# Chaining four of a pair's seven products in one PSUM bank, spilling intermediates unsplit, and putting TensorE's pages at one offset

## The chip, the cores and the metric

The kernel runs on one core of one Trainium2 chip. The metric is the device time of one execution in microseconds (us). The kernel before takes 2529.87 us, the median of three runs (2528.91 to 2531.84).

## The reference

A decoder block over 2048 positions of 1024 channels in float32: an RG-LRU group and a gated short convolution side by side, then a gated feed-forward part with a convolution, and a last norm.

```python
h = rms_norm(x, norm1_g);  z = h @ w_in            # 1024 -> 3584
y_lru = rg_lru(causal_dwconv(lru_x, 4 taps) + b, two gates of 64x64 blocks per head) * gelu(lru_gate)
y_sc  = sc_b * causal_dwconv(sc_c * sc_x, 3 taps)
x = x + concat(y_lru, y_sc) @ w_out                # 1536 -> 1024
h = rms_norm(x, norm2_g)
u = causal_dwconv(h @ w_up, 3 taps)                # 1024 -> 6144, halves gate and up
x = x + (gelu(gate) * up) @ w_down                 # 3072 -> 1024
out = rms_norm(x, final_g)
```

## The kernel before, in words

Channels lie on the 128 partitions and positions along the free axis. The 2048 positions are worked in two halves of T = 1024, since the scan and the convolutions run forward in time; a PSUM bank holds 512 positions (NB). Every product is made of three matmuls of 128x128 by 128x512 in the fp32r type: each operand is split into a high part, copied by ScalarE (ACT, line 147), and a remainder, subtracted by VectorE (DVE, line 148), and TensorE (PE) adds high by high, high by low and low by high (lines 152 and 176).

The phases follow one another on PE: input products of half 0 (tiles zin) with the gates (zr, zi) between them, output projection of half 0 (o), the same two of half 1, then for each half the up products (za to zd) and the down projection (d). A projection runs over two blocks of 512 positions; in a block all eight banks collect 1024 output channels over 12 steps (o) or 24 steps (d) of 24 matmuls. An up phase takes 24 pairs of a gate and an up channel block; a pair's 2x2 block product is done with seven products of 12 matmuls in a Winograd form (lines 526 to 572): sums of weights S1 to S4 are made on DVE from each pair's raw weights (line 513), sums of activations T1 to T4 once in h_prep. Before, three of the seven products have banks of their own or share one, and the partial results are put together by ACT copies (line 554) and DVE additions (line 550).

The order of PE's and SyncE's (SP) instructions is the order in which the program writes them; ACT, DVE and GpSimd (POOL) are put in order by a scheduler, in which high_priority moves work ahead by 120 (HP) or 90 (HW) places. SP starts the loads in that order, and an instruction that waits there holds all behind it. Stores of intermediates go through POOL's queue: y (12 tiles a half) and f (24 tiles a half) are split first, and both parts are written to DRAM (spill, line 234) and read back per block as yb; x2, x3 and half 0 of the output also leave by POOL.

Memory of PE's operands is in pages of 4 KB per partition: 28 act pages, 9 w pages (split weights, and the residuals xr, x2r of a projection), 5 tmp pages, 4 buffers tagged u of 4108 bytes (convolution inputs, loads of x and x2, and yb), 2 raw buffers of 5x512. In the built program the w pages lie at byte 2912 modulo 4096, the act pages at 3040, and the four u buffers at 2912, 2944, 2976 and 3008. So the address of the weights less that of the moving operand, modulo 512, is 384 for zin and for the up products, 0 for the gates (both in act pages), and 0, 480, 448 or 416 in turn for o and d, whose moving operand yb goes round the u buffers.

The mean of squares (inv_rms, line 195) of a norm is split on ACT and DVE and summed over partitions by four matmuls with a constant matrix (tiles ms). For the norms b and c this is written after the second unit or pair of the following phase (lines 628, 646 and 662), in one piece.

## Time and profile before

| what | value |
|---|---|
| median of three runs | 2529.87 us (2528.91 to 2531.84) |
| profiled execution, its own time | 2526.32 us |
| its span in the trace | 2524.6 us |
| PE busy | 2448.6 us (97%), 10,414 matmul rows |
| DVE busy | 1635.4 us (65%) |
| ACT busy | 1041.4 us (41%) |
| POOL busy | 250.6 us (10%) |
| mean granted TensorE clock | 0.984 |
| bytes moved by DMA | 368.89 MB, 274.88 on q1 (SP's) and 92.29 on q0 (POOL's) |

Where the phases lie, from the trace (us from the start of the span): input half 0 to 363, output 0 to 498, input half 1 to 844, output 1 to 986.6, up 0 to 1475, down 0 to 1742.6, up 1 to 2229.9, down 1 to 2524.6. A matmul's row lasts about 395 ns while the next starts some 232 ns after it, so the start-to-start distance and not the row's length is what a matmul costs in a stream. A granted clock below 1 in a stretch says that some of its matmuls ran at a lower clock.

### The profile page before, as it was taken

To read this page: it belongs to the slowest core of one execution; us is meant where nothing else is said; L and a number is where in the kernel's file an instruction comes from. 1 tells how busy PE (TensorE), PEld (TensorE's weight loads), DVE (VectorE), ACT (ScalarE), POOL (GpSimd) and SP (SyncE) were. 2 spreads that over 40 slices of the span, in tenths; PEclk is the share of its full clock that TensorE was granted. 3 is DMA by queue.
4 is the path that set the end of the run, shared out by engine and by line. 5 is a ranking of instruction groups with operands and counts; after the bars stand their busy time and mean duration, and the time that the engine had idled before them with its cause. 6 is when DMAs were issued, how large, how long until landed. Compare 5 with 4: busy or idle time off the path is not lost.

```text
span 2524.6 us, 26774 instructions
## 1 busy us (share of the span) xinstructions
PE 2448.6 (97%) x10414; PEld 1974.2 (78%) x10414; DVE 1635.4 (65%) x1753; ACT 1041.4 (41%) x1108; POOL 250.6 (10%) x379
## 2 busy tenths in 40 slices
PE   7999999999999998899999999999899999999996
PEld 5888887877888877688888888787688888888785
DVE  8555664556655666788888863534788888853423
ACT  5554453354554333444444432222444444431211
POOL 3100110000000000122211200000110011100000
PEclk9999999999999999999999999999999999999998
DMA  4222337713213475223332356754223322368554
GB/s 148 91 68 78 120 111 279 250 63 104 96 63 109 175 274 192 84 100 117 108 109 100 112 191 227 277 209 168 84 110 108 117 100 104 113 257 295 184 184 163
DMA packets 120064, 368.89 MB, mean 146 GB/s; under 512 B 10368, under 2 KB 13568, under 8 KB 119936
## 3 DMA queue, kind: packets, MB, share of 16 engines
q1 hardware_dynamic: 94592, 274.88, 31.8%
q0 software_dynamic: 25344, 92.29, 9.6%
q8 instruction: 82, 1.34, 0.2%
q14 instruction: 46, 0.38, 0.0%
HBM read 270.66 MB, written 96.47 MB: 145 GB/s over the span
## 4 chain that ended last, share of the span: by engine, by line
PE 93%; DVE 3%; DMA 2%; issue 1%; ACT 1%; SPq 0%; DVEq 0%; ACTq 0%
PE zin_b L178 24%; PE d L153 20%; PE za L539 11%; PE zd L539 11%; PE zc L539 11%; PE o L153 10%; PE zb L539 5%; PE zi_b L178 1%; PE zr_b L178 1%; DMA ybo<-y_d 1%; DMA ybd<-f_d 0%; DVE cv L232 0%; DMA wr_d<-in_w_down 0%; DMA ha<-x_d 0%; DMA x<-in_xT 0%
## 5 line engine op out<-in xcount | busy, mean ns | idle before, releaser
L153 PE MATMUL d<-ybd,wh_d 128*128 128x512 f32 x1536 | 482.3, 395 | 6.0 <-DMA ybd<-f_d 3.7
L153 PEld LDWEIGHTS d<-ybd,wh_d 128*128 128x128 f32 x1536 | 289.4, 189 | 75.0 <-issue 5.2
L153 PE MATMUL d<-ybd,wl_d 128*128 128x512 f32 x768 | 303.2, 395 | 0.0
L148 DVE TENSOR_TENSOR wl_d<-wr_d,wh_d 128x1024 fp32r<-128x1024 f32 x96 | 115.8, 1223 | 280.4 <-ACT wh_d L147 252.9
L178 PE MATMUL zin_b<-xl,wh_in 128*128 128x512 f32 x896 | 282.8, 397 | 6.5 <-DVE xl L334 6.5
L178 PE MATMUL zin_b<-xh,wh_in 128*128 128x512 f32 x896 | 283.5, 397 | 1.3 <-ACT xh L333 0.9
L178 PE MATMUL zin_b<-xh,wl_in 128*128 128x512 f32 x896 | 282.2, 396 | 0.0
L153 PE MATMUL o<-ybo,wh_o 128*128 128x512 f32 x768 | 242.5, 397 | 6.5 <-DMA ybo<-y_d 4.2
L147 ACT ACTIVATE wh_d<-wr_d 128x1024 fp32r<-128x1024 f32 x96 | 97.1, 1053 | 332.1 <-DMA wr_d<-in_w_down 318.7
L178 PEld LDWEIGHTS zin_b<-xl,wh_in 128*128 128x128 f32 x896 | 169.7, 190 | 47.5 <-DVE xl L334 7.8
L178 PEld LDWEIGHTS zin_b<-xh,wh_in 128*128 128x128 f32 x896 | 170.1, 190 | 42.3 <-ACT xh L333 1.5
L178 PEld LDWEIGHTS zin_b<-xh,wl_in 128*128 128x128 f32 x896 | 169.6, 189 | 39.9
L153 PEld LDWEIGHTS o<-ybo,wh_o 128*128 128x128 f32 x768 | 145.1, 190 | 41.8 <-issue 3.9
L153 PEld LDWEIGHTS d<-ybd,wl_d 128*128 128x128 f32 x768 | 145.0, 189 | 33.3
L153 PE MATMUL o<-ybo,wl_o 128*128 128x512 f32 x384 | 152.2, 396 | 0.7 <-DVE wl_o L148 0.7
L513 DVE TENSOR_TENSOR wr_up<-wr_up 128x512 f32<-128x512 f32 x192 | 132.2, 689 | 3.2
L148 DVE TENSOR_TENSOR wl_in<-wr_in,wh_in 128x1024 fp32r<-128x1024 f32 (+1 forms) x62 | 72.7, 1177 | 91.2 <-PE zin_b L178 85.6
L539 PE MATMUL zc<-hhB,whd_up 128*128 128x512 f32 x384 | 128.0, 394 | 0.0
L232 DVE SCALAR_TENSOR_TENSOR cg<-ug,prm,cg 128x1024 f32<-128x1024 f32 x96 | 122.7, 1279 | 3.0 <-issue 2.8
L232 DVE SCALAR_TENSOR_TENSOR cu<-un,prm,cu 128x1024 f32<-128x1024 f32 x96 | 122.6, 1277 | 0.0
L539 PE MATMUL zd<-ht,wha_up 128*128 128x512 f32 x384 | 120.5, 395 | 0.0
L554 ACT ACTIVATE ug<-za 128x512 f32<-128x512 f32 x96 | 56.7, 591 | 126.3 <-PE za L539 126.3
(236 smaller groups left out, 4587.7 us busy)
## 6 DMA issues: line engine op xcount, KB each, us to landing
wr_up<-in_w_up SPq DMA_DIRECT2D x96, 512.0 KB, 4.6
wr_d<-in_w_down SPq DMA_DIRECT2D x48, 1024.0 KB, 7.6
ybd<-f_d SPq DMA_DIRECT2D x96, 512.0 KB, 4.9
wr_in<-in_w_in SPq DMA_DIRECT2D x54, 512.0 KB, 3.6
wr_o<-in_w_out SPq DMA_DIRECT2D x24, 1024.0 KB, 6.9
ybo<-y_d SPq DMA_DIRECT2D x48, 512.0 KB, 5.6
f_d<-cg POOLq DMA_DIRECT2D x48, 512.0 KB, 3.1
f_d<-cu POOLq DMA_DIRECT2D x48, 512.0 KB, 3.1
```

Of the source, the lines that this page charges most:

```text
L147: nc.scalar.activation(r32(hi), src, AF.Copy)
L148: nc.vector.tensor_tensor(r32(lo), src, hi, ALU.subtract)
L153: nc.tensor.matmul(ps, r32(a), r32(b), start=(first and i == 0), stop=(last and i == 2))
L178: nc.tensor.matmul(ps[t], r32(a), r32(b[:, blk(t)]), start=(first and i == 0), stop=(last and i == 2))
L232: nc.vector.scalar_tensor_tensor(dst, src[:, k : k + T], col(o_w + k), dst, ALU.mult, ALU.add)
L513: nc.vector.tensor_tensor(raw[:, o, :], raw[:, a, :], raw[:, b, :], ALU.add)
L539: nc.tensor.matmul(ps, r32(p[:, s]), r32(hs[k][x][o]), start=f and i == 0, stop=l and i == 2, skip_group_check=True,)
L554: nc.scalar.activation(dst, ps, AF.Copy)
```

## The change

Several things change together.

**Up products.** A class, Pair, takes the place of up_products. Bank x collects W11, then S2, S3 and W22 on top of one another; ACT copies it out after each of the four, so that the partial sums serve as the common parts of the results. W12 has bank a, S1 and S4 share bank c. DVE makes three additions a pair where it made five, ACT four copies where it made two. A copy of bank x must be done before the next product writes into x.

On PE the order of the products changes. In the rows below, which are the first matmul of each product in the middle of the first up phase, the tile ahead of the arrow is the bank, the first name behind it the moving operand, the last the weights (wha holds W22 and W12, whb W11 and S2, whc S3 and S1, whd S4). The kernel before, pair 11 and the start of pair 12:

```order
L539 MATMUL za0_11_8015<-hhB110_0_5689,whb_up0_11_7865 128x512
...
L539 MATMUL zb0_11_8016<-hhT10_0_5697,whb_up0_11_7865 128x512
...
L539 MATMUL zd0_11_8017<-hhB110_0_5689,whc_up0_11_7871 128x512
...
L539 MATMUL zc0_11_8018<-hhT10_0_5697,whc_up0_11_7871 128x512
...
L539 MATMUL za0_11_8015<-hhB210_0_5693,wha_up0_11_7859 128x512
...
L539 MATMUL zd0_11_8017<-ht0_0_5701,wha_up0_11_7859 128x512 x2
...
L539 MATMUL zc0_11_8018<-hhB210_0_5693,whd_up0_11_7875 128x512
...
L539 MATMUL za0_12_8152<-hhB110_0_5689,whb_up0_12_8002 128x512
```

The changed kernel at the same place, from W11 of pair 11 on (S4 of pair 11, in zc, follows the last row):

```order
L567 MATMUL zx0_11_7933<-hhB110_0_5631,whb_up0_11_7875 128x512
...
L567 MATMUL zc0_11_7961<-hhT10_0_5639,whc_up0_11_7881 128x512
...
L567 MATMUL zx0_11_7933<-hhT10_0_5639,whb_up0_11_7875 128x512
...
L567 MATMUL za0_11_8034<-hhB210_0_5635,wha_up0_11_7869 128x512
...
L567 MATMUL zx0_11_7933<-hhB110_0_5631,whc_up0_11_7881 128x512
...
L567 MATMUL zx0_12_8066<-hhB110_0_5631,whb_up0_12_8008 128x512
...
L567 MATMUL zx0_11_7933<-ht0_0_5643,wha_up0_11_7869 128x512 x2
...
L567 MATMUL zc0_12_8094<-hhT10_0_5639,whc_up0_12_8014 128x512
```

Between S2 and S3 in bank x stands one product (W12), between S3 and W22 one (W11 of the next pair); between W11 and S2 stand three.

**Intermediates.** Y and f cross DRAM as they are, once. A projection reads the 512 positions that it needs (256 KB a step) into the raw tile of the weights, which grows from 5 to 6 half pages, and splits them there on ACT and DVE; the split yb lies in w pages (act pages in down 1).

**Stores.** All of POOL's stores move to SP's queue. defer(n, ...) puts one in a list, and tick, which runs after each load of weights, starts it n loads later (4 for y, 1 for f, x2, x3 and the output).

**Pages.** The u buffers get a pool of their own, w has 10 pages, tmp 6, and the scratch space of the software DMA queue shrinks from 16384 to 1024 bytes. In the built program all act and w pages then lie at byte 3936 modulo 4096, so that the weights' address less the moving operand's is 0 modulo 512 in every product; the u buffers lie at 3936 to 4032 and TensorE reads none of them.

**Smaller ones.** For the norms b and c the split of the sums (mean_split) is written one unit or pair ahead of the ms matmuls, at priority HP. A gate's weights are loaded and split a unit ahead. The residuals xr and x2r lie in u buffers instead of w pages. Half 1's x_prep and both halves' h_prep run at other steps of the projections. In up_rest the up channel's convolution comes first.

SP's rows at the end of up 0 and the start of down 0 (wr is a raw tile, in_w_down the weights, f_d the spilled f, cu its source) read before:

```order
L504 DMA wr_up0_23_9500<-in_w_up 128x2x512 x2
L387 DMA wr_d0_0_0_9761<-in_w_down 128x2x1024
L414 DMA ybd0_0_0_9771<-f_d0_0_106 128x1024
L414 DMA ybd0_0_1_9797<-f_d0_1_107 128x1024
L387 DMA wr_d0_0_2_9823<-in_w_down 128x2x1024
```

and now:

```order
L532 DMA wr_up0_23_9461<-in_w_up 128x2x512 x2
L157 DMA f_d0_21_130<-cu0_21_9452 128x1024
L408 DMA wr_d0_0_0_9682<-in_w_down 128x2x1024
L410 DMA wr_d0_0_0_9682<-f_d0_0_109 128x512
L410 DMA wr_d0_0_0_9682<-f_d0_1_110 128x512
L157 DMA f_d0_22_131<-cu0_22_9585 128x1024
L157 DMA f_d0_23_132<-cu0_23_9664 128x1024
L408 DMA wr_d0_0_2_9750<-in_w_down 128x2x1024
```

The stores of the last two pairs' f now stand ahead of the load for steps 2 and 3. Down 1 has the same order. At the border between the two blocks of a projection (here output 0) the four x2 stores stand ahead of the second load of the new block:

```order
L408 DMA wr_o0_1_0_2898<-in_w_out 128x2x1024
L410 DMA wr_o0_1_0_2898<-y_d0_0_85 128x512
L410 DMA wr_o0_1_0_2898<-y_d0_1_86 128x512
L157 DMA x2_d0_0_157<-xr0_0_0_2745 128x2x512
L157 DMA x2_d0_1_158<-xr0_0_1_2747 128x2x512
L157 DMA x2_d0_2_159<-xr0_0_2_2749 128x2x512
L157 DMA x2_d0_3_160<-xr0_0_3_2751 128x2x512
L408 DMA wr_o0_1_2_2968<-in_w_out 128x2x1024
```

Before, these stores were POOL's, and SP went from the loads of steps 0 and 1 to the next ones. The diff, cut to its core:

```diff
+    ub = ctx.enter_context(tc.tile_pool(name="ub", bufs=1))
...
-    y_d = [[dr.tile([P, 2, 2, NB], F32, name=f"y_d{h}_{k}") for k in range(NOUT)] for h in range(NH)]
-    f_d = [[dr.tile([P, 2, 2, NB], F32, name=f"f_d{h}_{k}") for k in range(NFF)] for h in range(NH)]
+    y_d = [[dr.tile([P, T], F32, name=f"y_d{h}_{k}") for k in range(NOUT)] for h in range(NH)]
+    f_d = [[dr.tile([P, T], F32, name=f"f_d{h}_{k}") for k in range(NFF)] for h in range(NH)]
...
-        return page(name, "w", 9)
+        return page(name, "w", 10)
...
-        return page(name, "tmp", 5)
+        return page(name, "tmp", 6)
...
-        return sb.tile([P, T + 3], F32, name=name, tag="u", bufs=4)
+        return ub.tile([P, T + 3], F32, name=name, tag="u", bufs=4)
...
-        return sb.tile([P, 5, NB], F32, name=name, tag="wr", bufs=2)
+        return sb.tile([P, 6, NB], F32, name=name, tag="wr", bufs=2)
...
+    waiting = []
+
+    def defer(n, dst, src):
+        waiting.append([n, dst, src])
+
+    def tick():
+        for w in waiting:
+            w[0] -= 1
+        while waiting and waiting[0][0] <= 0:
+            _, dst, src = waiting.pop(0)
+            nc.sync.dma_start(dst, src)
+
...
-        return next(load_parts(src, name, 1))
+        out = next(load_parts(src, name, 1))
+        tick()
+        return out
...
-    def inv_rms(acc, name):
+    def mean_split(acc, name):
...
-        pss = [pst(f"ms_{name}_{t}") for t in range(0, n, NB)]
...
-        split(hi, lo, acc)
+        with tc.high_priority(offset=HP):
+            split(hi, lo, acc)
+        return hi, lo
+
+    def inv_rms(acc, name, parts=None):
+        n = acc.shape[-1]
+        hi, lo = parts or mean_split(acc, name)
+        pss = [pst(f"ms_{name}_{t}") for t in range(0, n, NB)]
...
-    def lru_gates(c, half, xc):
+    def gate_weights(c, half):
...
-        split(hi, lo, raw)
+        with tc.high_priority(offset=HW):
+            split(hi, lo, raw)
+        return hi, lo
+
+    def lru_gates(c, half, xc, gw):
...
-            product_step(ps, wcol((hi, lo), g), xc, True, True)
+            product_step(ps, wcol(gw, g), xc, True, True)
...
+        gw = gate_weights(0, half)
...
-                gates = lru_gates(c, half, xc)
+                gates = lru_gates(c, half, xc, gw)
+                if c + 1 < NLRU:
+                    gw = gate_weights(c + 1, half)
...
-            spill(y_d[half][n], *(v.rearrange("p (t c) -> p t c", t=2) for v in y))
+            defer(4, y_d[half][n], y)
...
-    def load_k2(src, k, name):
+    def load_k2(src, spilled, t, k, name, ypage):
...
-        flat_raw = flat(raw)
-        nc.sync.dma_start(flat_raw[:, : 2 * T].rearrange("p (k m) -> p k m", k=2), src[k : k + 2].rearrange("k p m -> p k m"))
+        w = raw[:, 0:4, :].rearrange("p (k a) c -> p k (a c)", k=2)
+        nc.sync.dma_start(w, src[k : k + 2].rearrange("k p m -> p k m"))
+        for i in range(2):
+            nc.sync.dma_start(raw[:, 4 + i, :], spilled[k + i][:, blk(t)])
+        tick()
...
+            yb = ypage(f"yb_{name}_{k + i}")
...
-                split(hi, lo, flat_raw[:, i * T : (i + 1) * T])
-            out.append((hi, lo))
+                split(yb[:, 0, :], yb[:, 1, :], raw[:, 4 + i, :])
+                split(hi, lo, w[:, i, :])
+            out.append(((hi, lo), yb))
...
-                    wts = load_k2(src, k, f"{name}{half}_{t}")
-                yb = sb.tile([P, 2, NB], F32, name=f"yb{name}{half}_{t}_{k}", tag="u", bufs=4)
-                nc.sync.dma_start(yb, spilled[k][:, t, :, :])
+                    wts = load_k2(src, spilled, t, k, f"{name}{half}_{t}", act if last_k else wpage)
+                wt, yb = wts[k % 2]
...
+    def res_page(name):
+        return ub.tile([P, 2, NB], F32, name=name, tag="u", bufs=4)
+
...
-            r = wpage(f"xr{half}_{t}_{i}")
+            r = res_page(f"xr{half}_{t}_{i}")
...
-        nc.gpsimd.dma_start(dst[:, :, blk(t)].rearrange("m p c -> p m c"), r)
+        defer(1, dst[:, :, blk(t)].rearrange("m p c -> p m c"), r)
...
+        tick()
...
-    def up_products(half, j, wt, hs):
...
+    class Pair:
+        def __init__(self, half, j, hs):
+            self.half, self.j, self.hs = half, j, hs
+            self.wt = up_weights(half, j)
+            self.x, self.a, self.c = None, None, None
...
+        def copy(self, dst):
+            with tc.high_priority(offset=HP):
+                nc.scalar.activation(dst, self.x, AF.Copy)
+
+        def add(self, dst, ps):
+            with tc.high_priority(offset=HP):
+                nc.vector.tensor_tensor(dst, ps, dst, ALU.add)
...
+        def begin(self):
+            n = f"{self.half}_{self.j}"
+            self.ug = with_halo(f"ug{n}", 2, self.half, u_halo[:, self.j, :])
+            self.un = with_halo(f"un{n}", 2, self.half, u_halo[:, NFF + self.j, :])
+            self.g = [self.ug[:, 2 + b * NB : 2 + (b + 1) * NB] for b in range(2)]
+            self.n = [self.un[:, 2 + b * NB : 2 + (b + 1) * NB] for b in range(2)]
+            self.x = pst(f"zx{n}")
+            self.run(self.x, "W11", "B11", True, False)
+            self.copy(self.g[0])
+
+        def sum1(self):
+            self.c = pst(f"zc{self.half}_{self.j}")
+            self.run(self.c, "S1", "T1", True, False)
+
+        def middle(self):
+            self.run(self.x, "S2", "T2", False, False)
+            self.copy(self.g[1])
+            a = pst(f"za{self.half}_{self.j}")
+            self.run(a, "W12", "B21", True, True)
+            self.add(self.g[0], a)
+            self.run(self.x, "S3", "T3", False, False)
+            self.copy(self.n[1])
+            self.add(self.n[1], self.c)
+
+        def fourth(self):
+            self.run(self.x, "W22", "T4", False, True)
+            self.copy(self.n[0])
+            keep_halo(self.un, 2, self.half, u_halo[:, NFF + self.j, :])
+
+        def end(self):
+            self.run(self.c, "S4", "B22", False, True)
+            self.add(self.g[1], self.c)
+            keep_halo(self.ug, 2, self.half, u_halo[:, self.j, :])
...
+        conv(cu, un, 3, O_FCW + 3 * (NFF + j))
...
-        conv(cu, un, 3, O_FCW + 3 * (NFF + j))
...
-        split(cg, cu, cu)
-        spill(f_d[half][j], cg.rearrange("p (t c) -> p t c", t=2), cu.rearrange("p (t c) -> p t c", t=2))
+        defer(1, f_d[half][j], cu)
...
-        wt = up_weights(half, 0)
+        cur = Pair(half, 0, hs)
+        cur.begin()
+        cur.sum1()
...
-            nxt = up_weights(half, j + 1) if j + 1 < NFF else None
-            us = up_products(half, j, wt, hs)
-            up_rest(half, j, *us)
-            wt = nxt
+            nxt = Pair(half, j + 1, hs) if j + 1 < NFF else None
+            cur.middle()
+            if nxt is not None:
+                nxt.begin()
+            cur.fourth()
+            if nxt is not None:
+                nxt.sum1()
+            cur.end()
+            up_rest(half, j, cur.ug, cur.un)
+            cur = nxt
...
-        if s % 2 == 0 and 4 <= s < 4 + 2 * KC:
+        if s in (4, 5, 6, 7, 16, 17, 18, 19):
...
-    def in1_between(n):
-        if n == 1:
-            rs2[0] = inv_rms(ss2[0], "b0")
+    def late_mean(acc, name, out, first):
+        held = []
...
-    in_phase(1, x1, ss1[1], in1_between)
+        def between(n):
+            if n == first:
+                held.append(mean_split(acc, name))
+            elif n == first + 1:
+                out.append(inv_rms(acc, name, held[0]))
+
+        return between
+
+    in_phase(1, x1, ss1[1], late_mean(ss2[0], "b0", rs2[0], 1))
...
-            if s >= first and (s - first) % every == 0 and len(hs[half]) < 4:
-                hs[half].append(h_prep(half, len(hs[half]), rs2[half]))
+            if s in at:
+                hs[half].append(h_prep(half, len(hs[half]), rs2[half][0]))
...
+    project(1, NOUT, w_out, y_d[1], "o", x_residual(1), out_done(1), h_beside(0, (3, 6, 16, 18)))
...
-    up_phase(0, hs[0], up0_between)
+    up_phase(0, hs[0], late_mean(ss2[1], "b1", rs2[1], 1))
...
+    project(0, NFF, w_down, f_d[0], "d", x2_residual(0, res_page), down0_done, h_beside(1, (4, 10, 15, 30)))
...
-    up_phase(1, hs[1], up1_between)
+    rs3 = []
+    up_phase(1, hs[1], late_mean(ss3, "c0", rs3, 1))
...
-                nc.gpsimd.dma_start(yT[2 * i + m, :, 0:T], flat(t))
+                defer(1, yT[2 * i + m, :, 0:T], flat(t))
...
-    nc = bacc.Bacc("TRN2", target_bir_lowering=False, num_devices=1)
+    nc = bacc.Bacc("TRN2", target_bir_lowering=False, num_devices=1, dynamic_dma_scratch_size=1024)
```

## The prediction, made before the changed kernel was run

> **What bounds the kernel now.** I read the page first, for the shares and the chain of waits.

> ```profile
> PE 2448.6 (97%) x10414; PEld 1974.2 (78%) x10414; DVE 1635.4 (65%) x1753; ACT 1041.4 (41%) x1108; POOL 250.6 (10%) x379
> ...
> PE 93%; DVE 3%; DMA 2%; issue 1%; ACT 1%; SPq 0%; DVEq 0%; ACTq 0%
> ```

> TensorE is the bound in every phase. So two things can move the time: what a matmul costs in a stream, and the stretches in which PE starts none. For the first I read the chain in order of time, which puts uninterrupted runs of matmuls in one row (start, length, what, count).

> ```profile
> 257.10 55.79 PE zin_b L178 x240
> ...
> 363.04 44.27 PE o L153 x192
> ...
> 1051.23 2.79 PE zd L539 x12
> ...
> 1475.09 110.95 PE d L153 x480
> ```

> Length by count gives the start-to-start distance: 232.5 ns for zin, 232.5 for an up product, 230.6 for o, 231.1 for d. All are 128x128 by 128x512 at full granted clock, yet they differ. The timeline of PE inside output 0 shows where from (start, length, instruction, count).

> ```profile
> 447.97 0.62 PE L153 MATMUL o<-ybo,wh_o 128*128 128x512 f32 x2
> ...
> 453.56 0.63 PE L153 MATMUL o<-ybo,wh_o 128*128 128x512 f32 x2
> ...
> 454.94 0.61 PE L153 MATMUL o<-ybo,wh_o 128*128 128x512 f32 x2
> ...
> 459.02 0.63 PE L153 MATMUL o<-ybo,wh_o 128*128 128x512 f32 x2
> ```

> 447.97 and 453.56 are the first matmuls of two successive steps: 24 matmuls in 5.59 us, 232.9 ns each. In the second step 18 matmuls lie between 454.94 and 459.02: 4.08 us, 226.7 ns each. The weights come from the same kind of page in both; the moving operand yb lies in another u buffer. In the first step the address difference (weights less moving, modulo 512) is 480, in the second 0; zin and up, at 384, stand at 232.5. So I read the distance as set by that difference: 226.7 ns at 0, about 233 elsewhere.

> For the second thing, the waits of PE (waiting line, releaser: total us, times, longest) and windows around the longest (from:to, length, busy us and count of PE, PEld, DVE, ACT and POOL, granted clock, DMA share, GB/s).

> ```profile
> PE za L539 <- ACT whb_up L147: 8.7, 2, 4.4
> ...
> PE o L153 <- DMA ybo<-y_d: 4.2, 2, 2.4
> PE ms_c L202 <- ACT rh_c L147: 4.0, 1, 4.0
> PE ms_b L202 <- ACT rh_b L147: 4.0, 1, 4.0
> PE ms_b L203 <- DVE rl_b L148: 4.0, 1, 4.0
> PE ms_c L203 <- DVE rl_c L148: 3.8, 1, 3.8
> PE d L153 <- DMA ybd<-f_d: 3.7, 2, 2.5
> ```

> ```profile
> 986.60:996.40 9.80, 5.30 (x13) 3.38 (x12) 9.69 (x15) 4.70 (x5) 1.73 (x4) 0.67 0.57 215
> 1033.00:1047.70 14.70, 6.69 (x17) 4.67 (x16) 12.89 (x14) 7.80 (x8) 2.69 (x5) 0.66 0.32 120
> 1742.60:1750.70 8.10, 3.38 (x9) 1.85 (x9) 7.99 (x13) 3.65 (x4) 1.66 (x3) 0.81 0.52 196
> 1788.20:1802.10 13.90, 6.13 (x16) 4.17 (x15) 12.06 (x13) 7.80 (x8) 5.45 (x4) 0.64 0.28 108
> 893.70:907.70 14.00, 10.94 (x40) 7.96 (x39) 11.43 (x12) 6.41 (x7) 0.00 (x0) 0.89 0.90 341
> 965.80:972.70 6.90, 4.53 (x14) 3.25 (x13) 0.56 (x1) 1.65 (x2) 0.09 (x1) 0.76 1.02 400
> 2481.20:2488.30 7.10, 4.61 (x14) 3.31 (x14) 0.69 (x1) 0.63 (x1) 0.00 (x0) 0.77 0.96 346
> 1103.00:1298.20 195.20, 195.20 (x842) 158.28 (x841) 169.03 (x190) 89.89 (x100) 40.58 (x60) 1.00 0.30 108
> ```

> What a stretch loses is its length less its matmuls at 0.2325 us: 10.7 us for 1033.0 (14.70 - 17 x 0.2325), though PE waited only 4.0 + 4.0 there. The granted clock of 0.66 says why: after the waits matmuls run at a lower clock for some time, so 8.0 us of waiting cost 10.7. The other rows lose 6.8, 6.0, 10.2, 4.7, 3.6 and 3.8 us. The last row, ten pairs, loses nothing: there the distance alone counts.

> **The change part by part.**

> Pages. The change puts every pair of operands at difference 0. Matmuls by the program: zin 56 products of 48 = 2688, up 48 pairs of 84 = 4032, o 1152, d 2304. At 226.7 ns: zin 2688 x 5.8 = 15.6 us, up 4032 x 5.8 = 23.4, o 1152 x 3.9 = 4.5, d 2304 x 4.4 = 10.1. Together -53.6. Bounds: 0 if the address has nothing to do with it, -54 if all is as in the one step; I take -53.6, because the two steps follow each other and do the same work on the same kind of weight page. [...]

> Norms b and c. The rows of the first wait:

> ```profile
> 1036.32 1.04 ACT L147 ACTIVATE rh_b<-ss_b 128x1024 fp32r<-128x1024 f32 x1
> ...
> 1037.41 0.55 PE L202 MATMUL ms_b<-rh_b,ones_r 128*128 128x512 f32 x1 [4.01 <-ACT rh_b L147]
> ...
> 1040.69 1.22 DVE L148 TENSOR_TENSOR rl_b<-ss_b,rh_b 128x1024 fp32r<-128x1024 f32 x1
> ```

> The split's two instructions stand behind the pair's own work on ACT and DVE, and PE is already there. Now they are written a pair (19 us) ahead of the ms matmuls, at high priority. Both losses go: -(10.7 + 10.2), and I leave +1 for what the split displaces: -20.

> Starts of the up phases (6.8 + 6.0 lost, PE waits for whb_up). The residuals no longer hold w pages, so the first pair's splits can run before the last additions of the projection. But four x stores now precede pair 1's load on SP. I leave 2.2 us each: -8.4. Bounds: -12.8 and 0.

> Projections. The waits for ybo, ybd and ha (4.7 + 3.6 + 3.8 us in the windows, and the second waits in the rows of ybo, 4.2 - 2.4, and ybd, 3.7 - 2.5, another 3) go: y and f come with the weights, in half the bytes, into other buffers. New at the block borders of o0, o1 and d0: the load for steps 2 and 3 is behind four stores that wait for the last additions.

> ```profile
> wr_d<-in_w_down SPq DMA_DIRECT2D x48, 1024.0 KB, 7.6
> wr_o<-in_w_out SPq DMA_DIRECT2D x24, 1024.0 KB, 6.9
> ```

> Two DVE additions of 0.69 us a store pair let it start some 2 us into the block, it lands 7 to 7.6 later, and the split takes 1 to 2: 11 to 12 us, while PE needs it after 48 x 0.2267 = 10.9. That is 0 to 1 us of waiting plus lower clock, 3 us each, 9 in all. Bounds 0 and 15. Net -6.

> Starts of down 0 and down 1. Here the same load is behind the stores of f 22 and f 23, and the last f is only finished inside the down phase. Before, at T = 1475.1:

> ```profile
> 1463.69 0.39 SPq L387 DMA_DIRECT2D wr_d<-in_w_down  x1
> ...
> 1476.52 0.68 DVE L550 TENSOR_TENSOR ug<-zc,ug 128x512 f32<-128x512 f32 x1
> ...
> 1477.29 1.15 ACT L228 ACTIVATE cg<-ug,prm 128x1024 f32<-128x1024 f32 x1 [2.73 <-issue]
> ...
> 1480.92 1.28 DVE L232 SCALAR_TENSOR_TENSOR cg<-ug,prm,cg 128x1024 f32<-128x1024 f32 x1
> ...
> 1482.24 1.06 ACT L577 ACTIVATE cg<-cg 128x1024 f32<-128x1024 f32 x1 [2.76 <-DVE cg L232]
> ...
> 1483.51 1.23 DVE L579 SCALAR_TENSOR_TENSOR cu<-cg,cu 128x1024 f32<-128x1024 f32 x1
> ```

> The load started 11.4 us before T. Now it waits for the product in the last row, which ended at T + 9.6. With cu's taps written first: addition to T + 2.1, scale 3.3, two taps 5.9, gelu 7.0, product 8.3. SP starts the load at T + 8.8, it lands at T + 16 to 17, split until T + 18 to 19; PE has used up steps 0 and 1 at T + 10.9. So 8 us of waiting, and by 1033.0 (8.0 waited, 10.7 lost) 11 us lost, twice: +22. Bounds: 10, if the load lands in 4 us, and 28.

> Up phases in the steady state. Per ten pairs (groups of 1103.0 to 1298.2: count, busy us, mean ns):

> ```profile
> L550 DVE TENSOR_TENSOR un<-zd,ug 128x512 f32<-128x512 f32 x20 | 13.8, 688 | 0.0
> L148 DVE TENSOR_TENSOR cu<-cu,cg 128x1024 fp32r<-128x1024 f32 x10 | 12.1, 1214 | 0.0
> L554 ACT ACTIVATE ug<-za 128x512 f32<-128x512 f32 x20 | 11.8, 589 | 25.8 <-PE za L539 25.8
> L147 ACT ACTIVATE cg<-cu 128x1024 fp32r<-128x1024 f32 x10 | 10.6, 1063 | 6.1 <-DVE cu L579 6.1
> ```

> DVE loses two additions and f's split, 16.9 - 1.4 - 1.2 = 14.3 us of a pair of 84 x 0.2267 = 19.0; ACT gains two copies and loses f's split, about 9.1 of 19.0. Both have room. What is new is the chain in bank x: S3 waits for the copy after S2, W22 for the copy after S3, with one product, 12 x 0.2267 = 2.72 us, between them. A copy takes 0.59, so ACT may be 2.1 us late. Walking ACT's new order through a pair I find it late by one split at most (1.06): 0.9 to 1.3 us to spare. Cost 0, but in the last pair no product covers the copy: 0.9 x 2 = +2. Bounds: 0, and the rivals below. Gates, POOL's emptied queue, the scratch space: 0, y is started some 20 us after it is ready and f is not read before the phase ends.

> Sum: -53.6 - 20 - 8.4 - 6 + 22 + 2 = -64.0. The span of 2524.6 becomes 2460.6. The runs' median is 5.3 above that span (2529.87 - 2524.6; the profiled execution itself took 2526.32), so 2466.

> **The rivals.**

> B. The load behind f 22 and f 23 costs little, because the last f is ready earlier or the landing is quicker. For it: before, the taps had to queue with weight splits that now come later. Against it: SP's order. 2466 - 22 = 2444.

> C. The chain in bank x costs a little in every pair. For it: two copies with 1 us to spare in an order that a scheduler made. 0.5 us x 48 = +24: 2490.

> D. The distance does not follow the addresses; the 226.7 ns come from something else of that buffer. For it only that 0 is seen in short runs. 2466 + 53.6 = 2520.

> E, slower than before. ACT reaches each of the two tight copies behind a scale, a gelu and a split, 1.15 + 1.06 + 1.06 = 3.3 us, 1.1 more than the 2.1: 2.2 us a pair, 48 pairs, +106: 2572. It decides from 1.4 us a pair on (64 / 48 = 1.3 to come back to before). Against it: ACT is busy 89.9 of 195.2 us in the row of ten pairs.

> **How the numbers follow.** Forecast 0.50, B 0.20, C 0.15, D 0.09, E 0.06. The likeliest is 2466. B to C spans 2444 to 2490; to that I add half of what the bounds of the up starts and the borders leave (4.4 and 9 below, 8.4 and 6 above): 2437 to 2497, which leaves out D, E and little more. About 0.2% (5 us) is what a measurement of this kernel tells from no change. Faster: all but E and a part of D with other losses, 0.93; same 0.02; slower 0.05.

> **What would show it.** Uninterrupted runs of zin, up, o and d at 226.7 ns in the chain (a zin run of 240 in 54.4 us, a pair in 19.0); if they stay at 232.5, the page term is wrong. No waits of ms_b and ms_c of 4 us. A wait of d of about 8 us some 11 us into both down phases, released by wr_d or the split behind it, and SP waiting for cu. No wait of the up products for a copy of ACT; if there is one in each pair, C or E holds. The prediction falls if the steady up phase is longer than 19.1 us a pair.

## The result

The changed kernel takes 2457.4 us (median of four runs, 2453.78 to 2458.68), the one before 2529.39 (four runs). The ratio is 0.9711, with a 95% interval of 0.9694 to 0.9728. The forecast was 2466 us with a range of 2437 to 2497. The span of the profiled execution went from 2524.6 to 2452.0 us, by 72.6.

The page of the changed kernel, busy time of the engines and the chain by engine:

```profile
span 2452.0 us, 26367 instructions
...
PE 2389.5 (97%) x10414; PEld 1965.8 (80%) x10414; DVE 1572.9 (64%) x1729; ACT 1106.8 (45%) x1276; POOL 100.4 (4%) x203
...
PE 88%; DVE 6%; DMA 2%; issue 2%; ACT 2%; SPq 0%; DVEq 0%; ACTq 0%; POOL 0%
```

PE still starts the same matmuls, and its busy time fell by 59 us. Where that comes from shows in the chain in order of time (start, length, what, count):

```profile
250.16 54.40 PE zin_b L193 x240
...
431.23 54.24 PE o L166 x238
...
1044.66 2.72 PE zx L567 x12
1047.38 2.72 PE za L567 x12
1050.10 8.16 PE zx L567 x36
1058.26 5.44 PE zc L567 x24
1063.70 2.72 PE zx L567 x12
...
1571.74 108.45 PE d L166 x477
```

240 matmuls of zin take 54.40 us, 226.7 ns each (232.5 before). The runs of o and d come to 227.9 and 227.4 by their counts; each begins right behind a short wait at a block border, with a first distance of 338 ns (o) and 335 ns (d) and the next ones at 224 to 236 ns, while the last ones are 226 to 227 ns. A pair of the up phase takes 1063.70 - 1044.66 = 19.04 us, and no row of a copy stands between its products. Over all start-to-start distances under 260 ns, which leaves out the waits and the matmuls at the lower clock (426 to 427 ns apart behind the wait of down 0), the mean is 226.66 ns (10,263 of them), before 231.93 (10,250): 54 us.

The waits of PE after the change (waiting line, releaser: total us, times, longest):

```profile
PE zin_b L193 <- ACT wh_in L160: 7.0, 2, 3.5
PE zx L567 <- DVE wlb_up L161: 6.2, 4, 2.6
...
PE d L166 <- ACT wh_d L160: 5.2, 2, 5.0
PE d L166 <- ACT yb_d L160: 3.9, 1, 3.9
...
PE zx L567 <- ACT un L578: 1.4, 2, 0.7
```

The waits of ms_b and ms_c and those for ybo and ybd are gone. In their place d waits at the start of both down phases and zx in the up phases; at the starts of the input phases zin now waits for its weights (7.0 us in all), where before zr waited for the gates' (8.9 us). Windows around the new ones (from:to, length, busy us and count of PE, PEld, DVE, ACT and POOL, granted clock, DMA share, GB/s):

```profile
1431.40:1441.60 10.20, 5.17 (x13) 3.39 (x12) 4.80 (x6) 5.11 (x7) 0.00 (x0) 0.67 1.01 385
1026.00:1036.00 10.00, 7.23 (x25) 5.25 (x24) 9.50 (x12) 5.30 (x6) 1.11 (x1) 0.83 0.45 140
1704.00:1712.00 8.00, 6.21 (x19) 4.33 (x19) 5.91 (x8) 3.40 (x5) 0.00 (x0) 0.79 0.00 0
1766.00:1773.50 7.50, 4.93 (x16) 3.44 (x15) 7.03 (x8) 2.85 (x4) 0.00 (x0) 0.77 0.59 203
2168.50:2179.00 10.50, 6.01 (x15) 4.10 (x14) 5.24 (x6) 5.81 (x8) 0.00 (x0) 0.68 1.01 383
428.50:432.00 3.50, 2.69 (x11) 1.61 (x10) 2.74 (x4) 2.88 (x4) 0.00 (x0) 1.00 1.03 413
898.00:902.00 4.00, 2.61 (x11) 1.54 (x10) 2.79 (x4) 3.05 (x4) 0.00 (x0) 1.00 1.04 412
1569.50:1572.50 3.00, 2.23 (x9) 1.25 (x8) 2.73 (x4) 2.40 (x3) 0.00 (x0) 1.00 0.94 376
968.00:972.00 4.00, 2.63 (x11) 1.56 (x10) 2.84 (x5) 1.55 (x2) 0.24 (x1) 1.00 0.00 0
```

Length less 0.2267 us for each matmul gives what each loses: 7.3 and 7.1 us at the starts of down 0 and down 1 (first and fifth row), 4.3 and 3.9 in the up phases near the norms (second and fourth), 1.5 and 3.7 at the starts of up 0 and up 1 (last and third), 1.0, 1.5 and 1.0 at the block borders.

### The profile page after: what moved, and what is told of

Read it like the earlier page. It is cut to its first block, busy times and chain, and to the rows that moved or that the text cites. A ratio compares the mean times of both kernels' runs of the same rounds, so it can differ in the third digit from the quotient of the medians.

```text
span 2452.0 us, 26367 instructions
## 1 busy us (share of the span) xinstructions
PE 2389.5 (97%) x10414; PEld 1965.8 (80%) x10414; DVE 1572.9 (64%) x1729; ACT 1106.8 (45%) x1276; POOL 100.4 (4%) x203
## 4 chain that ended last, share of the span: by engine, by line
PE 88%; DVE 6%; DMA 2%; issue 2%; ACT 2%; SPq 0%; DVEq 0%; ACTq 0%; POOL 0%
PE zin_b L193 24%; PE zx L567 20%; PE d L166 19%; PE zc L567 10%; PE o L166 10%; PE za L567 5%; PE zi_b L193 1%; PE zr_b L193 1%; DMA wr_up<-in_w_up 1%; DMA wr_d<-f_d 1%; DVE x2r L466 1%; DVE cg L253 1%; DVE wr_up L542 0%; DVE wl_in L161 0%; DVE xr L466 0%
## 5 line engine op out<-in xcount | busy, mean ns | idle before, releaser
L166 PE MATMUL d<-yb_d,wh_d 128*128 128x512 f32 x1536 | 479.1, 393 | 12.1 <-ACT wh_d L160 5.2
L166 PEld LDWEIGHTS d<-yb_d,wh_d 128*128 128x128 f32 x1536 | 291.6, 190 | 74.9 <-ACT wh_d L160 6.1
L166 PE MATMUL d<-yb_d,wl_d 128*128 128x512 f32 x768 | 301.5, 393 | 0.6 <-DVE wl_d L161 0.5
L166 PE MATMUL o<-yb_o,wh_o 128*128 128x512 f32 x768 | 236.8, 389 | 1.2 <-ACT wh_o L160 1.2
L166 PEld LDWEIGHTS d<-yb_d,wl_d 128*128 128x128 f32 x768 | 145.8, 190 | 32.3 <-DVE wl_d L161 1.7
L166 PEld LDWEIGHTS o<-yb_o,wh_o 128*128 128x128 f32 x768 | 144.0, 188 | 31.7 <-ACT wh_o L160 2.0
L166 PE MATMUL o<-yb_o,wl_o 128*128 128x512 f32 x384 | 149.6, 390 | 1.1 <-DVE wl_o L161 1.1
L249 ACT ACTIVATE cg<-ug,prm 128x1024 f32<-128x1024 f32 x48 | 55.3, 1153 | 164.6 <-DVE ug L582 164.6
L567 PE MATMUL zx<-ht,wha_up 128*128 128x512 f32 x384 | 118.5, 390 | 1.4 <-ACT un L578 1.4
L160 ACT ACTIVATE wh_in<-wr_in 128x1024 fp32r<-128x1024 f32 (+1 forms) x62 | 59.9, 973 | 108.9 <-DMA wr_in<-in_w_in 99.4
## 6 DMA issues: line engine op xcount, KB each, us to landing
wr_d<-in_w_down SPq DMA_DIRECT2D x48, 1024.0 KB, 5.1
wr_o<-in_w_out SPq DMA_DIRECT2D x24, 1024.0 KB, 6.6
```

The costliest lines, as they stand in the source:

```text
L160: nc.scalar.activation(r32(hi), src, AF.Copy)
L166: nc.tensor.matmul(ps, r32(a), r32(b), start=(first and i == 0), stop=(last and i == 2))
L249: nc.scalar.activation(dst, src[:, last : last + T], AF.Copy, scale=col(o_w + last))
L567: nc.tensor.matmul(ps, r32(p[:, s]), r32(self.hs[k][x][o]), start=f and i == 0, stop=l and i == 2, skip_group_check=True,)
```

## The experiments

Each is set against runs of the kernel before on the same chip (medians 2526.8, 2529.7 and 2529.1 us in the three groups), so the ratios are what is compared. What a trace loses is from here on the excess of the start-to-start distances over the plain one. It comes out 0.2 to 0.5 us higher at a place than by the windows above, which also count matmuls that they cut: the 4.7 and 4.2 us in the texts below are the 4.3 and 3.9 above.

### Do the addresses set the matmul's distance?

Theory P: the address difference modulo 512 sets the distance. Rival D: something else does. The first kernel takes the alignment out of the changed one for some products, with the others as a control inside the same run.

```diff
     def act(name):
+        if not padded:
+            padded.append(sb.tile([P, 32], F32, name="pad", tag="pad", bufs=1))
+            nc.gpsimd.memset(padded[0], 0.0)
         return page(name, "act", 28)
```

> The changed kernel with the act pages moved up by 128 bytes, so that the difference between weights and moving operand is 384 modulo 512 again for zin, for all up products and for down 1 (whose yb lies in act pages), and stays 0 for both output projections and down 0 (yb in w pages). Theory P (the address difference sets the distance): zin, zx, zc, za and d of down 1 go back to 232.5 ns, o and d of down 0 stay at 226.7; 7872 matmuls x 5.8 ns = +45.7, so 2503 us (2497 to 2509). Rival D (the distance does not follow the addresses): all stay at 226.7, 2457 us.

Measured: 2497.52 us, ratio 0.9878 (0.9858 to 0.9897), at the lower end of what P gives. The chain in order of time:

```profile
258.44 55.79 PE zin_b L198 x240
...
364.39 60.58 PE o L171 x267
...
1089.34 8.40 PE zx L572 x36
```

and 100 us inside down 0 and inside down 1 (windows, columns as above):

```profile
1480.00:1580.00 100.00, 100.00 (x443) 82.82 (x442) 55.59 (x63) 39.59 (x50) 0.00 (x0) 1.00 0.50 182
2240.00:2340.00 100.00, 100.00 (x430) 80.47 (x429) 42.99 (x49) 30.38 (x39) 0.00 (x0) 1.00 0.60 215
```

zin is back at 232.5 ns, zx at 233.3; o stays at 226.9 with its yb in w pages. In the same time and with PE busy throughout, down 0 (yb in w pages) starts 443 matmuls, down 1 (yb in act pages) 430; over all distances under 260 ns d has 226.7 in the one and 232.9 in the other. P holds, D falls: nothing but 128 bytes of padding, and POOL's one instruction that clears them, was added.

The second puts the alignment alone into the kernel before.

```diff
+    ub = ctx.enter_context(tc.tile_pool(name="ub", bufs=1))
...
-        return sb.tile([P, T + 3], F32, name=name, tag="u", bufs=4)
+        return ub.tile([P, T + 3], F32, name=name, tag="u", bufs=4)
...
-                yb = sb.tile([P, 2, NB], F32, name=f"yb{name}{half}_{t}_{k}", tag="u", bufs=4)
+                yb = ub.tile([P, 2, NB], F32, name=f"yb{name}{half}_{t}_{k}", tag="u", bufs=4)
```

> The kernel before with nothing changed but the u buffers in a pool of their own behind the act pages, which brings act and w pages to the same offset modulo 512 (zin and up at difference 0; yb of o and d goes round the four differences as before). Theory P: zin and the up products at 226.7 ns, 6720 x 5.8 = -39.0, the waits of before unchanged: 2490 us (2486 to 2494). Rival D: 2529 us, zin and up at 232.5.

Measured: 2487.14 us, ratio 0.9836 (0.9819 to 0.9853), which is some 40 us less. Its chain and waits:

```profile
252.04 54.40 PE zin_b L179 x240
...
355.40 44.22 PE o L154 x192
...
1001.42 2.72 PE zd L540 x12
```

```profile
PE ms_c L203 <- ACT rh_c L148: 4.0, 1, 4.0
PE ms_b L204 <- DVE rl_b L149: 4.0, 1, 4.0
```

zin and the up products are at 226.7 ns, o with its four buffers still at 230.3, and the 4-us waits of the norms are as before. So the placement of pages alone is worth some 40 us in the old kernel, and it does not change the waits.

The third spreads the act pages.

```diff
     def act(name):
-        return page(name, "act", 28)
+        t = sb.tile([P, 2 * NB + 8], F32, name=name, tag="act", bufs=28)
+        return t[:, : 2 * NB].rearrange("p (a b) -> p a b", a=2)
```

> The changed kernel with act pages 4128 bytes apart instead of 4096, so that the difference between weights and moving operand takes all sixteen multiples of 32 modulo 512 in zin, the up products and down 1. Theory P: the distance is a function of the difference alone: 226.7 ns at 0, about 229 at 448 and 233 at 416, 480 and 384 (the differences that the kernel before had), the rest not known; time between 2457 and 2510 us. Rival: only pages that share their offset modulo 4096 are fast, so that all differences but 0 stand at 232 to 233: 2505 us.

Measured: 2491.5 us, one run. The distances under 260 ns of its trace, by the address difference of the matmul in the built program (mean in ns, count):

```
  0: 227.8 (2937)    32: 232.6 (227)    64: 232.2 (278)    96: 231.6 (222)
128: 230.6 (310)    160: 232.5 (604)   192: 230.4 (550)   224: 231.0 (430)
256: 231.5 (727)    288: 232.4 (569)   320: 232.1 (516)   352: 233.0 (608)
384: 231.8 (527)    416: 232.4 (634)   448: 230.7 (582)   480: 232.9 (532)
```

These means are no price of a single difference. In zin and the up products of this kernel nearly every difference lasts for one to three matmuls, and there a matmul at 0 is hardly faster than the others (zin: 230.8 ns at 0, 231.9 elsewhere). The 227.8 ns at 0 come from o and down 0, which keep 0 throughout and give 2352 of the 2937 distances. Down 1 tells more, because a step there keeps one difference for 24 matmuls. Here are a step at 256 and the one behind it, at 288, each from its tenth matmul on:

```profile
2316.75 0.62 PE L167 MATMUL d<-yb_d,wh_d 128*128 128x512 f32 x2
...
2319.47 0.62 PE L167 MATMUL d<-yb_d,wh_d 128*128 128x512 f32 x2
...
2322.25 0.63 PE L167 MATMUL d<-yb_d,wh_d 128*128 128x512 f32 x2
...
2325.05 0.63 PE L167 MATMUL d<-yb_d,wh_d 128*128 128x512 f32 x2
```

From the first row to the second twelve matmuls take 2.72 us, 226.7 ns each, and from the third to the fourth 2.80 us, 233.3 ns each. From the tenth matmul on all such steps of down 1 come to 226.7 ns at 0 and at 256 (three steps each), 229.0 at 192, 229.9 at 448 (228.6 to 228.9 in three steps, 233.4 in the fourth), and 232.6 to 234.3 at the eleven other differences that occur (352 does not). So the values that P names are met where a difference lasts, the rival falls at 256, and in these steps the pattern repeats after 256 bytes and not after 512. It is also not the difference of a matmul alone: in the kernel before, the gates, at 0 amid a stream at 384, took 231.4 ns (zr) and 228.9 ns (zi), and in the changed kernel, still at 0, 227.1 and 226.8.

### Is it SP's order that costs the new waits?

The next kernel stores f two loads later instead of one.

```diff
-        defer(1, f_d[half][j], cu)
+        defer(2, f_d[half][j], cu)
```

> The changed kernel with f stored two loads later instead of one, so that on SP the load for steps 2 and 3 of a down phase stands ahead of the stores of f 22 and f 23, and in the up phase a pair's load ahead of the f store that it followed. Theory S (SP's order makes the wait at the start of the down phases): the load is issued some 10 us before the phase, the waits of d (7.7 and 7.3 us lost) go, -15: 2442 us; the losses of 4.7 and 4.2 us in pairs 2 and 3 of the up phases go too if they come from a load behind an f store (2433), and stay if they come from the norm's own work on ACT and DVE. Rival T (the load is late because the DMA queues are full there, not because of the order): less than 4 us of change, 2455 us.

Measured: 2430.39 us, ratio 0.9613 (0.9595 to 0.963), 27 us less than the changed kernel by the two medians, 24.8 by the two ratios. SP's timeline of the changed kernel around the start of down 0 (PE's first d matmul is at 1420.90), and of this one:

```profile
1396.32 0.39 SPq L408 DMA_DIRECT2D wr_d<-in_w_down  x1
...
1413.89 14.79 SPq L157 DMA_DIRECT2D f_d<-cu  x2
1428.78 0.38 SPq L408 DMA_DIRECT2D wr_d<-in_w_down  x1
```

```profile
1379.97 0.39 SPq L408 DMA_DIRECT2D wr_d<-in_w_down  x1
...
1396.07 0.32 SPq L157 DMA_DIRECT2D f_d<-cu  x1
1399.01 0.38 SPq L408 DMA_DIRECT2D wr_d<-in_w_down  x1
...
1414.35 16.23 SPq L157 DMA_DIRECT2D f_d<-cu  x2
1430.68 0.38 SPq L408 DMA_DIRECT2D wr_d<-in_w_down  x1
```

The first load of each is that for steps 0 and 1, the second that for steps 2 and 3. In the changed kernel SP stands at the two f stores from 1413.89 to 1428.7, and only then starts the second load. Now that load leaves at 1399.01, and the 16 us at the stores hold only the third. The chain has an unbroken row from the first step on:

```profile
1421.52 125.81 PE d L166 x555
```

The losses in pairs 2 and 3 went too (0.1 us each left): a pair's raw weights had been behind an f store. That is the first of the two sub-cases, theory S with 2433; rival T falls.

Then all the deferred stores go back to POOL's queue; y and f stay unsplit.

```diff
     def defer(n, dst, src):
-        waiting.append([n, dst, src])
+        nc.gpsimd.dma_start(dst, src)
```

> The changed kernel with all its deferred stores back on GpSimd's queue, issued when their data is written in the program; y and f stay unsplit. Theory S (what the changed kernel loses at the starts of the down phases, in pairs 2 and 3 and at the block borders is SP's order alone): -15 - 9 - 4: 2429 us (2425 to 2436), as e_f2 or a little better. Rival: GpSimd's queue with the small scratch space is slow, and y or f come late: waits of o or d for DMA, over 2445 us.

Measured: 2421.03 us, ratio 0.9568 (0.9554 to 0.9582), better than expected. The losses at the starts of the up phases, which the expectation had left in, are gone as well. So moving the stores to SP cost some 36 us of the changed kernel (0.9711 against 0.9568), and POOL's queue with 1024 bytes of scratch space shows no wait of its own:

```profile
PE zin_b L193 <- ACT wh_in L160: 7.0, 2, 3.5
PE zin_b L193 <- DVE xl L352: 6.2, 2, 6.0
PE ms_l L223 <- ACT rh_l L160: 3.7, 2, 2.8
PE zr_b L193 <- DVE xcl L161: 3.3, 2, 1.6
```

The last of this group stays on SP, with f, x2, x3 and the output two loads late and the first gate's weights loaded later.

```diff
-        gw = gate_weights(0, half)
+        gw = None
...
+                if gw is None:
+                    gw = gate_weights(0, half)
                 gates = lru_gates(c, half, xc, gw)
...
-        defer(1, f_d[half][j], cu)
+        defer(2, f_d[half][j], cu)
...
-        defer(1, dst[:, :, blk(t)].rearrange("m p c -> p m c"), r)
+        defer(2, dst[:, :, blk(t)].rearrange("m p c -> p m c"), r)
```

> As e_f2, and x2, x3 and the output are stored two loads later as well, and the first gate's weights of a half are loaded behind the first load of input weights that follows instead of ahead of it. Theory S: the losses at the block borders (1.3, 1.5 and 0.9 us) and half of those at the up starts (3.8 and 2.2) go, -6; the load of input weights no longer stands on SP behind the gate weights, which wait for the page that the norm's matmuls read, so that half of the losses at the start of the input phases (6.6 and 7.7) go, -7: 2417 us (2412 to 2424). Rival: those waits have another cause (the split on ScalarE behind the norm's own work), 2425 us or more.

Measured: 2422.10 us, ratio 0.9572 (0.9557 to 0.9586). The borders and the up starts lose nothing any more, all of it rather than half. The gate part failed: zin no longer waits for wh_in at the start, but zr waits for gw instead,

```profile
PE zr_b L193 <- ACT gw L160: 9.4, 2, 4.7
```

and the starts of the input phases lose 9.6 and 9.7 us around the gates, about what zin and zr together lost. Moving that load changed which wait is last, not the loss. That the time still lies inside the expected range is the work of the borders and the up starts, which gave more than the 6 us expected, and so partly luck.

### What does the chain in one bank bring?

As e_f2, with up_products and up_phase of the kernel before in place of the class Pair (their code stands above).

```diff
-        cur = Pair(half, 0, hs)
-        cur.begin()
-        cur.sum1()
+        wt = up_weights(half, 0)
         for j in range(NFF):
...
+            nxt = up_weights(half, j + 1) if j + 1 < NFF else None
+            us = up_products(half, j, wt, hs)
+            up_rest(half, j, *us)
+            wt = nxt
             between(j)
```

> As e_f2 (f stored two loads later), but with the up products of the kernel before: seven products in four banks, five additions on VectorE and two copies on ScalarE, no product of the next pair ahead of time. Theory N (VectorE is not the bound in the up phases, so the chain in one bank brings no time): no loss in the steady pairs, the wait of the last pair for its copy (1.0 and 1.4 us) gone, up to 3 us more at the norms, where no product of the next pair covers: 2428 to 2434 us against 2430 for e_f2. Rival V (the chain is what lets VectorE keep up): waits of the up products in each pair, 0.2 us a pair or more, 2440 us or more.

Measured: 2423.70 us, ratio 0.9579 (0.9563 to 0.9595), a little better than the lower end of theory N; rival V falls. The up products show no wait at all, and the losses at the starts of the up phases (3.8 and 2.2 us in e_f2) are gone too, because no product of the next pair is needed early there. Together with POOL's queue, that is with this edit beside it and f's stores as in the changed kernel:

```diff
     def defer(n, dst, src):
-        waiting.append([n, dst, src])
+        nc.gpsimd.dma_start(dst, src)
```

> The changed kernel with the up products of the kernel before (no chain in one bank, no product of the next pair ahead of time) and with all deferred stores on GpSimd's queue. If the two gains are of different places (the chain: the last pairs' copies, 1.0 and 1.4 us; SP's order: up starts, pairs 2 and 3, block borders, starts of down): 2421 - 2.4 = 2418 us (2415 to 2421). If the chain has a cost of its own in the steady pairs: 2413 or less.

Measured: 2417.57 us, ratio 0.9558 (0.9545 to 0.9571), the fastest kernel of this study. Against e_pool1024 (0.9568) the intervals overlap, so a gain of 3 us is only what the two traces show: spans of 2415.0 and 2418.4, with the 1.0 and 1.4 us of the last pairs gone. The chain gave the time nothing in either queue arrangement.

### What do the unsplit intermediates bring?

```diff
-        defer(1, f_d[half][j], cu)
+        split(cg, cu, cu)
+        spill(f_d[half][j], cg.rearrange("p (t c) -> p t c", t=2), cu.rearrange("p (t c) -> p t c", t=2))
...
-        for i in range(2):
-            nc.sync.dma_start(raw[:, 4 + i, :], spilled[k + i][:, blk(t)])
...
-                split(yb[:, 0, :], yb[:, 1, :], raw[:, 4 + i, :])
+                nc.sync.dma_start(yb, spilled[k + i][:, t, :, :])
```

(y likewise, on top of e_pool1024.)

> As e_pool1024, but y and f are split before they are stored and cross DRAM as two parts, as in the kernel before (both parts stored on GpSimd's queue, read back by SP straight into the yb page). Pages, order of the loads and buffers stay those of e_pool1024. Theory H (half the bytes removed the waits of o and d for yb, 12 to 15 us with lower clock): 2421 + 12 = 2433 us (2427 to 2440), waits o <- yb and d <- yb for DMA in the trace. Rival I (the waits went because yb has other buffers, loaded earlier; the bytes do not matter): 2421 us (2418 to 2425).

Measured: 2422.54 us, ratio 0.9576 (0.9563 to 0.9589), against 0.9568 with unsplit data: no difference that can be measured. The bytes are those of the kernel before again, and no wait for yb is among PE's waits:

```profile
HBM read 270.66 MB, written 96.47 MB: 152 GB/s over the span
```

So rival I holds: halving the bytes did not remove the waits for ybo and ybd. What did is in what this kernel shares with the changed one; of these (other buffers for yb, loads with the weights, residuals in other pages) the runs single out none.

### What does the early split of the norms bring?

```diff
             if n == first:
-                held.append(mean_split(acc, name))
-            elif n == first + 1:
-                out.append(inv_rms(acc, name, held[0]))
+                out.append(inv_rms(acc, name))
```

and without the raised priority of the split; first in the changed kernel, then in e_final.

> The changed kernel with the split of the sums of norms b and c again written in one piece with their ms matmuls, at no raised priority. Theory N (the early split removed two waits of 8 us, which cost 10.7 and 10.2): the waits ms <- rh and ms <- rl come back, +21 at most; less the 4.7 and 4.2 us that the changed kernel loses in the same pairs, if those only moved: +12, so 2469 to 2478 us. Rival (PE has other work between, since two products of the next pair now stand ahead of the ms matmuls): under 4 us, 2457 to 2461.

Measured: 2463.05 us, ratio 0.9741 (0.9723 to 0.9758) against 0.9711: some 6 to 8 us, between the theory and its rival. The waits of ms come back smaller (3.0 + 1.0 and 3.5 + 0.7 us), and the losses of 4.7 and 4.2 us near them go.

> As e_final, with the split of the sums of norms b and c in one piece with their ms matmuls, at no raised priority. With PE in the order of the kernel before, theory N expects the two waits back at their old size (8 us each, 10.7 and 10.2 lost): e_final + 20, 2438 us (2434 to 2442). Rival (in the changed kernel's place the split is ready early whatever its priority): e_final + 4 or less.

Measured: 2434.51 us, ratio 0.9624 (0.9611 to 0.9637) against 0.9558 for e_final, 17 us. Theory N holds in kind; the rival falls. The waits:

```profile
PE ms_c L222 <- ACT rh_c L160: 3.5, 1, 3.5
PE ms_b L222 <- ACT rh_b L160: 3.5, 1, 3.5
PE ms_c L223 <- DVE rl_c L161: 1.4, 1, 1.4
PE ms_b L223 <- DVE rl_b L161: 1.1, 1, 1.1
```

The split's ACT part is as late as before the change, its DVE part less so (1.1 and 1.4 us, where it was 4.0 and 3.8). So the two waits cost 7.6 and 7.8 us, not 10.7 and 10.2.

## Why the prediction was right, term by term

| term | predicted us | measured us | from |
|---|---|---|---|
| pages | -53.6 | -54 | 10,250 distances, 231.93 to 226.66 ns |
| norms b and c | -20 | -12.7 | 20.9 lost before gone, 4.3 + 3.9 new |
| starts of the up phases | -8.4 | -7.6 | 12.8 before, 1.5 + 3.7 left |
| projections | -6 | -11.6 | 15.1 before, 1.0 + 1.5 + 1.0 left |
| starts of the down phases | +22 | +14.4 | 7.3 + 7.1 |
| last pairs' copies | +2 | +2 | waits of 1.4 in all, the distance behind each 339 and 338 ns |
| sum | -64.0 | -69.5 | span -72.6 |

The remaining 3 us are not broken down. The terms agree less well than the sum: the starts of the down phases and the projections came out 7.6 and 5.6 us better than forecast and the norms 7.3 us worse, so part of the closeness of the sum is luck. The runs' median stands 5.4 us above the span, 5.3 was taken.

**Pages.** Right in mechanism and size, and shown from both sides: taken out by 128 bytes, put into the old kernel by moving one pool. The bound of 0, that the address has nothing to do with it, did not come true: the same matmuls, apart only in where their pages lie, take 232.5 or 226.7 ns. What in the hardware makes the differences 0 and 256 fast, no run here shows. "About 233 elsewhere" was too wide: in the kernel before, o and d at 448 had 229.5 ns (812 distances). The sum does not suffer, since it took o and d by their measured means. And 0 in every product holds for all but the few ms matmuls, which lie at 256; in the changed kernel they too start 226.7 ns apart.

**Starts of the down phases.** The mechanism was right: SP at the f stores, the load behind them, PE out of weights after two steps. The loss was a third smaller than forecast. With T = 1420.90, the start of down 0, the product was finished at 1428.3 (T + 7.4, against 8.3) and the load issued at T + 7.9; it landed 6.1 us later and not 7 to 8, and PE went on at T + 16 instead of 18 to 19. It waited 5.0 us, not 8.

**Starts of the up phases.** The size was right. The 5.2 us that are left take two things together, the x stores ahead of pair 1's load on SP and the chain's early product of pair 1: nothing is lost there in e_pool1024 and e_best, where the stores are out of the way, nor in e_unchain2, without the chain. Whether it is the pages of the residuals that removed the rest, as the prediction has it, no run singles out.

**Norms.** The two waits went, as said, but the term left out that the same f stores which hold the down phases also hold the loads of pairs 2 and 3; there the norm's own work on ACT and DVE (two table loads of 1.28 us each on ACT, four more DVE instructions of 3.7 us together, at norm b) meets raw weights that came late, and 8.2 us come back. In e_f2, where the loads leave earlier, they are gone, and in e_norm, where the split is late, they are gone too: it takes the early split and the load behind the f store together. "I leave +1 for what the split displaces" was the step that failed.

**Projections.** "In half the bytes" was no reason: e_split moves all the bytes and waits for none. The borders cost 1.0 to 1.5 us each and not 3: the longest single wait of o there was 0.9 us, and the rows show a granted clock of 1.00, so the lower clock that the term counted on did not come.

**Steady up phase.** The walk through ACT's order was right: 19.04 us a pair, no wait for a copy, so rivals C and E fell. But the chain brings nothing either, and at the starts and ends of the up phases it costs (3.8 and 2.2 us, 1.0 and 1.4 us in e_f2).

**Rivals.** B (the f stores cost little) would have been 2444; e_f2 shows that price at 25 us with the up pairs in it. D fell with e_shift and e_balign.

## What to carry to other kernels

Before arguing about waits, look at what one matmul costs in an unbroken stream, product by product: a difference of 2.5% between products of one shape (232.5 against 226.7 ns), which changed with the buffer, was an address effect here, and a pad or another order of pools is worth a try. A store on SP's queue held every load behind it until its data was ready (14.79 us at the start of down 0); give such a store to another queue, or write it behind the loads that are due first. And a change with several parts may win by one of them: here the pages gave 54 us and the early norms 6 to 8 (17 in the fastest kernel, with the stores off SP's queue), the queue took 36 back, and the chain and the unsplit intermediates gave nothing.
